# The first step of a hybrid decoder layer: one interleaved chain of products for 512 tokens, or four chains of 128 tokens each

## The chip, the cores and the metric

The kernel runs on one core of a Trainium2 chip. The core has a matrix engine (TensorE, PE in the profile; its weight loads are PEld), a vector engine (VectorE, DVE), a scalar engine (ScalarE, ACT), a general engine (GpSimd, POOL) and an engine that issues most DMAs (SyncE, SP). PE, DVE and ACT work between two on-chip memories: SBUF, with 128 partitions, and PSUM, with eight banks of 128x512 float32 into which PE writes. The metric is the device time of one execution in microseconds.

## What is computed

One decoder layer on 1024 tokens of width 1024, in float32. The change touches only the beginning of it, the normalization and the large input projection:

```python
def rms_norm(x, g):
    xf = x.astype(jnp.float32)
    y = xf * lax.rsqrt(jnp.mean(xf * xf, axis=-1, keepdims=True) + NORM_EPS)
    return (y * g.astype(jnp.float32)).astype(x.dtype)

def hybrid_layer(x, layer_idx, pre_g, post_g, w_in, ...):
    h = rms_norm(x, pre_g)
    z = jnp.einsum('bsd,de->bse', h, w_in)
    qa, ka, va, ga, qb, kb, vb, gb, gk_low = split_columns(z)
    ...
```

Behind it come causal differential softmax attention (8 heads), chunked gated linear attention (4 heads), gates, and an output projection with a second normalization and the residual.

## The kernel before

**Products in three terms.** Every float32 operand of a large product is split into a high part, rounded to a narrower format (a copy, on ACT mostly), and a low part, the operand less the high part (a subtraction, on DVE). A product is then hi*hi + hi*lo + lo*hi. In the profile `h_hi`, `s_hi`, `w` are written by CAST, COPY or ACTIVATE on ACT, their low parts by TENSOR_TENSOR on DVE. One call of `mm` (L144) is one product of a 128x128 stationary and a 128x512 moving operand; `tr` (L147) is a transpose of 128x128.

**Seven products for eight.** The projection of a column group is done on 2x2 blocks, tokens in halves of 512 and width in halves of 512, with a scheme of Strassen's kind: steps n = 1 to 7 of a column group p multiply one combination of activation blocks (h11, h12, h22, s1 to s4) by one combination of weight blocks (b11, b12, b21, b22). Step n=1 is h11 times b11, n=2 is h12 times b21, n=5 is s1 times b12 - b11, n=6 s2 times b11 - b12 + b22 (built up in place), n=7 s3 times b22 - b12. The list `order` sets which (p, n) follow each other: (0,1), (1,1), (0,2), (1,2), (2,1), (2,2), then n = 5, 6, 7, 4 for p = 0 and 1 in turn. Columns p = 0 and 1 are the values of the gated part: there the tokens are the stationary operand, one PSUM bank for each of four tiles of 128 tokens (the results x and y in the profile; their sums go out as gv_st through `take_gated`). p = 2 is the first ordinary group; its weights come through `w_early`.

**The first step.** `load_x` (L675) loads x in eight tiles of 128 tokens. SP's queue holds x0 to x3, b11's first half, pre_g, b11's second half, x4 to x7, b21, w_early. `norm_x` takes the mean square of a tile (ACT, into `junk`; for tile 3 half of it on DVE), adds eps (DVE), takes the power -0.5 (POOL, `ssq`), and `scale_x` multiplies the tile by it (DVE). `first(0)` transposes the first 512 columns of the four tiles into four banks, one bank for each 128 columns, with spins (products of zeros) between to fill PE's wait; `put` multiplies by pre_g, by now along partitions, while it makes the high part (ACT) and the low part (DVE). `gated_first` then runs the products of all four tiles interleaved: 16 of w_hi with h_hi, 16 of w_hi with h_lo, then `first(1)`, 16 transposes for the other half of the columns (h12, through the float copy `f1`, in the profile f), then 16 with w_lo.

**The second half of the tokens.** `blocks(j)`, for j = 0 to 3, transposes column block j and j+4 of tiles 4 to 7 (8 transposes), scales them with pre_g (ACT, the tiles t21 and t22, both t in the profile) and makes s1 = h21 + h22 (DVE). blocks(0) stands ahead of (0,2), blocks(1) behind it, blocks(2) behind (1,2), blocks(3) behind (2,1). `differences(j)` then makes h21 = h11_hi - h21, adds h11_lo, and s2 = h22 less that, all on DVE. s4 = f1 - s2 follows in front of (0,7), again on DVE.

**What sets the order.** The engines run in order. PE's instructions keep the program's order. While `pinned[0]` is set, the instructions of ACT, DVE and POOL keep it too (L56 to L59); later ones are placed by a scheduler, with `tc.issue_after` as hints. `hold` limits how far `prepare` may make weights ahead, and `between` keeps pieces of work for a later place. `free` hands PSUM banks out in turn.

Of the kernel before, what the change touches and what calls it, by code (L numbers as in the profile page):

```python
# [31 lines left out]
def hymba_kernel(  # L32
# [288 lines left out]
    def gated_weights(n):  # L321
# [26 lines left out]
        if n == 1:  # L348
            for k in range(2):
                dve.tensor_copy(w[0][:, k], src[0][:, k])  # L350
            between[:] = [
                lambda: lo(1),
                lambda: (scale_x(3, cols(1)), lo(0)),
                lambda: act.copy(w[1][:, 1], src[1][:, 1]),
                lambda: (act.copy(w[1][:, 0], src[1][:, 0]), scale_x(2, cols(1))),
                lambda: [scale_x(st, cols(1)) for st in range(2)],
            ]
# [1489 lines left out]
```

## Time and profile before

| what | value |
| --- | --- |
| median of 3 runs | 961.26 us (960.8 to 961.41) |
| the profiled execution | 960.34 us |
| its span, from the first to the last instruction | 958.6 us |
| PE, PEld busy | 948.2 us (99%), 793.2 us (83%) |
| DVE, ACT, POOL busy | 742.3 us (77%), 604.7 us (63%), 193.9 us (20%) |
| TensorE clock granted | 0.998 |

The span stands 1.74 us below the profiled execution's time; 1.74 us lie around it. All durations come from this one execution. Busy shares are means over the whole span; the change concerns its first 80 us. In rows of the timeline the first number is the start in microseconds from the span's start and the second the length; "x4" counts instructions, and in brackets stands how long the engine was idle before the row and which engine's work ended that.

### The profile page before, as it was taken

To read this page: it belongs to the slowest core of one execution; us is meant where nothing else is said; L and a number is where in the kernel's file an instruction comes from. 1 tells how busy PE (TensorE), PEld (TensorE's weight loads), DVE (VectorE), ACT (ScalarE), POOL (GpSimd) and SP (SyncE) were. 2 spreads that over 40 slices of the span, in tenths; PEclk is the share of its full clock that TensorE was granted. 3 is DMA by queue.
4 is the path that set the end of the run, shared out by engine and by line. 5 is a ranking of instruction groups with operands and counts; after the bars stand their busy time and mean duration, and the time that the engine had idled before them with its cause. 6 is when DMAs were issued, how large, how long until landed. Compare 5 with 4: busy or idle time off the path is not lost.

```text
span 958.6 us, 14358 instructions
## 1 busy us (share of the span) xinstructions
PE 948.2 (99%) x4624; PEld 793.2 (83%) x4624; DVE 742.3 (77%) x1476; ACT 604.7 (63%) x1162; POOL 193.9 (20%) x263
## 2 busy tenths in 40 slices
PE   9999999999999999999999999999999999999997
PEld 7877788888888888888888888888888888888885
DVE  5998799996778787687767476588888888898464
ACT  7753355845777556577765444366677677787773
POOL 2001002222141112131100002122222222433321
PEclk9999999999999999999999999999999999999999
DMA  8546367487577897986755498996665679994776
GB/s 285 162 149 172 91 203 244 168 293 249 188 255 242 275 305 255 295 258 216 263 175 154 143 298 265 411 291 217 220 223 193 222 230 349 331 291 105 160 206 141
DMA packets 153258, 220.34 MB, mean 230 GB/s; under 512 B 15776, under 2 KB 85664, under 8 KB 153088
## 3 DMA queue, kind: packets, MB, share of 16 engines
q1 hardware_dynamic: 138736, 177.65, 57.8%
q0 software_dynamic: 14448, 41.79, 14.8%
q8 instruction: 36, 0.59, 0.3%
q14 instruction: 38, 0.31, 0.1%
HBM read 133.93 MB, written 88.60 MB: 232 GB/s over the span
## 4 chain that ended last, share of the span: by engine, by line
PE 96%; DVE 1%; ACT 1%; DMA 1%; issue 0%; POOL 0%; SPq 0%; DVEq 0%; ACTq 0%
PE x L144 23%; PE z L144 16%; PE y L144 16%; PE ypart L144 14%; PE sc L144 7%; PE po L144 5%; PE yps L144 4%; PE wtr L147 3%; PE gpo L144 3%; PE kv L144 1%; PE gkl_ps L144 1%; PE pa L144 1%; PE xT L147 1%; DMA x<-in_x_dram 1%; PE ms L144 0%; PE pk L147 0%
## 5 line engine op out<-in xcount | busy, mean ns | idle before, releaser
L66 ACT CAST w<-w_raw 128x512 fp32r<-128x512 f32 x138 | 85.1, 620 | 70.0 <-PE y L144 31.7
L66 ACT ACTIVATE p<-p,stt 128x896 f32<-128x896 f32 (+7 forms) x128 | 99.3, 777 | 30.8 <-DVE stt L66 29.9
L66 DVE TENSOR_TENSOR w<-w_raw,w 128x512 fp32r<-128x512 f32 x138 | 94.0, 684 | 31.5 <-ACT w L66 31.4
L66 ACT COPY s<-x 128x512 f32<-128x512 f32 x78 | 44.7, 584 | 65.1 <-PE x L144 64.9
L66 DVE CUSTOM_DVE_ANT_0 p<-sc,maskt 128x512 f32<-128x512 f32 (+3 forms) x128 | 74.2, 585 | 14.5 <-PE sc L144 13.2
L66 POOL TENSOR_SCALAR p<-p,stt,lam 128x1024 f32<-128x1024 f32 (+3 forms) x64 | 55.9, 874 | 143.9 <-DVE stt L66 143.8
L144 PE MATMUL z<-s_hi,w 128*128 128x512 f32 x320 | 80.1, 393 | 0.0
L144 PE MATMUL x<-s_hi,w 128*128 128x512 f32 x320 | 80.0, 392 | 0.0
L144 PE MATMUL y<-h_hi,w 128*128 128x512 f32 x320 | 80.0, 392 | 0.0
L144 PE MATMUL ypart<-wo_hi,m_hi 128*128 128x512 f32 x192 | 79.5, 414 | 0.1
L144 PE MATMUL ypart<-wo_hi,m_lo 128*128 128x512 f32 x192 | 75.5, 393 | 0.0
L144 PE MATMUL ypart<-wo_lo,m_hi 128*128 128x512 f32 x192 | 75.4, 393 | 0.0
L66 POOL DMA_DIRECT2D wo_d<-wo_hi x32 | 17.4, 543 | 270.4 <-ACT wo_hi L66 270.4
L144 PEld LDWEIGHTS z<-s_hi,w 128*128 128x128 f32 x320 | 59.8, 188 | 12.3
L144 PEld LDWEIGHTS x<-s_hi,w 128*128 128x128 f32 x320 | 59.7, 188 | 12.3
L144 PEld LDWEIGHTS y<-h_hi,w 128*128 128x128 f32 x320 | 59.7, 188 | 12.2
L144 PE MATMUL sc<-k,q 128*128 128x512 f32 (+1 forms) x192 | 68.9, 362 | 0.1
L144 PE MATMUL sc<-ks,q 128*128 128x512 f32 (+1 forms) x192 | 66.1, 347 | 0.0
L66 ACT CAST wt_hi<-wtr 128x512 fp32r<-128x512 f32 (+1 forms) x80 | 42.8, 534 | 29.0 <-PE wtr L147 28.3
L66 DVE TENSOR_TENSOR wt_lo<-wtr,wt_hi 128x512 fp32r<-128x512 f32 (+1 forms) x80 | 50.6, 633 | 9.9 <-ACT wt_hi L66 9.1
L66 DVE TENSOR_TENSOR w_raw<-w_raw 128x512 f32<-128x512 f32 x80 | 56.2, 703 | 1.4 <-DMA w_raw<-in_w_in_dram 0.4
L66 DVE TENSOR_TENSOR c<-z,s 128x512 f32<-128x512 f32 x48 | 32.8, 687 | 31.3 <-ACT s L66 19.3
(234 smaller groups left out, 2348.0 us busy)
## 6 DMA issues: line engine op xcount, KB each, us to landing
w_raw<-in_w_in_dram SPq DMA_DIRECT2D x40, 512.0 KB, 4.9
wo_d<-wo_hi POOLq DMA_DIRECT2D x32, 256.0 KB, 3.0
q<-q_d SPq DMA_DIRECT2D x32, 256.0 KB, 5.3
k<-k_d SPq DMA_DIRECT2D x32, 256.0 KB, 5.5
ks<-k_d SPq DMA_DIRECT2D x64, 128.0 KB, 6.2
wo_raw<-in_w_out_dram POOLq DMA_DIRECT2D x31, 256.0 KB, 5.0
v<-v_d SPq DMA_DIRECT2D x14, 512.0 KB, 7.7
wo_d<-gqd POOLq DMA_DIRECT2D x22, 256.0 KB, 4.1
```

Source lines behind the costliest of these rows:

```text
L66: ins = op(*a, **k)
L144: tc.keep_in_program_order(pe.matmul(*a, **k))
L147: tc.keep_in_program_order(pe.transpose(dst, src, ident))
```

## The change

**Loads.** SP's queue now holds x0, g_bc, x1, b11 in both halves, x2, x3, x4, pre_g, b21, x5 to x7, w_early. g_bc is new: the first 512 numbers of the pre-norm weights, broadcast to 128 partitions (256 KB).

**Four chains.** Each tile of 128 tokens goes through the start by itself: mean square, power, one DVE instruction that multiplies its first 512 columns by the norm and by g_bc (`scale_g`), four transposes into one bank (`turn_x`), two casts of 128x2x128 for the high part (`put_hi`), two subtractions for the low part (`put_lo`), and twelve products into its own bank (`products`). Tile 1's transposes stand behind four products of tile 0. b11's low part is made on DVE between tile 1's and tile 2's. `second_half` (formerly `first(1)`) follows tile 3's transposes; its 16 transposes stand ahead of tile 3's twelve products.

**The rest.** The squares of tiles 5, 6 and 7 come behind the casts of h12. Tiles 6 and 7 are scaled by ACT. blocks(0) moves into step (1,2), behind its first chain, blocks(1) behind that step, blocks(2) and blocks(3) behind (2,1). The low weights of (0,5) are made behind blocks(3). The four additions of h11_lo in `differences` and the four subtractions from f1 go from DVE to POOL. The casts of s4 get a hint that places them behind the weight casts of (0,7).

At PE's start before, all transposes come first (`x_188` holds tiles 0 and 1, `x_191` tiles 2 and 3):

```order
L144 MATMUL spin<-idle,ones 128x512 x13
L147 MATMUL xT<-ident,x_188 128x128 x4
L144 MATMUL spin<-idle,ones 128x512 x3
L147 MATMUL xT<-ident,x_188 128x128 x4
L144 MATMUL spin<-idle,ones 128x512 x5
L147 MATMUL xT<-ident,x_191 128x128 x8
L144 MATMUL spin<-idle,ones 128x512
L144 MATMUL x<-w,h_hi 128x512 x16
L144 MATMUL x<-w,h_lo 128x512 x16
```

PE's start with the change (`x_199` holds tiles 2 and 3):

```order
L144 MATMUL spin<-idle,ones 128x512 x13
L147 MATMUL xT<-ident,x_188 128x128 x4
L144 MATMUL spin<-idle,ones 128x512 x5
L144 MATMUL x<-w,h_hi 128x512 x2
L144 MATMUL x<-w,h_lo 128x512 x2
L147 MATMUL xT<-ident,x_188 128x128 x4
L144 MATMUL x<-w,h_hi 128x512 x2
L144 MATMUL x<-w,h_lo 128x512 x2
L144 MATMUL x<-w,h_hi 128x512 x4
L144 MATMUL x<-w,h_lo 128x512 x4
L144 MATMUL x<-w,h_hi 128x512 x4
L147 MATMUL xT<-ident,x_199 128x128 x4
```

Products of tile 0 now stand ahead of the transposes of the other tiles, and tile 1's products ahead of tile 2's transposes.

On DVE from the first sum s1 of `blocks` before (`t_416` is t21, `t_417` t22, `s_428` and `s_492` the first two sums, `g_raw<-g_raw` the subtractions b12 - b11, gv_st the sums of y and x):

```order
L66 TENSOR_TENSOR s_428<-t_416,t_417 128x512
L66 TENSOR_TENSOR g_raw<-g_raw 128x1024
L66 TENSOR_TENSOR w<-w_early,w 128x512 x2
L66 TENSOR_TENSOR gv_st<-y,s 128x512
L66 TENSOR_TENSOR g_raw<-g_raw 128x1024
L66 TENSOR_TENSOR t_416<-h_hi,t_416 128x512
L66 TENSOR_TENSOR s_lo<-s_428,s_hi 128x512
L66 TENSOR_TENSOR gv_st<-y,s 128x512
L66 TENSOR_TENSOR w<-g_raw,w 128x1024
L66 TENSOR_TENSOR s_492<-t_416,t_417 128x512
L66 TENSOR_TENSOR t_416<-h_lo,t_416 128x512
L66 TENSOR_TENSOR gv_st<-y,s 128x512
```

The same place with the change (`t_459` is t21, `t_460` t22):

```order
L66 TENSOR_TENSOR gv_st<-y,s 128x512 x2
L66 TENSOR_TENSOR w<-w_early,w 128x512 x2
L66 TENSOR_TENSOR s_491<-t_459,t_460 128x512
L66 TENSOR_TENSOR g_raw<-g_raw 128x1024 x2
L66 TENSOR_TENSOR gv_st<-y,s 128x512
L66 TENSOR_TENSOR t_459<-h_hi,t_459 128x512
L66 TENSOR_TENSOR gv_st<-y,s 128x512
L66 TENSOR_TENSOR s_lo<-s_491,s_hi 128x512
L66 TENSOR_TENSOR w<-g_raw,w 128x1024
L66 TENSOR_TENSOR s_535<-t_459,t_460 128x512
L66 TENSOR_TENSOR w<-g_raw,w 128x1024
```

The first two gv_st now stand ahead of the first sum, the third behind the sum and both g_raw subtractions, and the additions of h_lo (`t_416<-h_lo,t_416`) are no longer there.

On POOL, from the two last powers to the first large fill, with the change (before, the two DMAs and the MEMSET followed each other, with nothing between):

```order
L66 TENSOR_TENSOR ssq<-ssq,eps_t 128x2 x2
L66 TENSOR_TENSOR t_459<-h_lo,t_459 128x512 x2
L66 DMA gk_up<-in_w_gk_up_dram 16x512
L66 TENSOR_TENSOR t_459<-h_lo,t_459 128x512 x2
L66 DMA wd<-in_w_in_dram 128x8x16
L66 TENSOR_TENSOR s_624<-f_353,s_624 128x512 x2
L66 TENSOR_TENSOR s_625<-f_353,s_625 128x512 x2
L66 MEMSET gkl 128x1024
```

The eight operations taken from DVE stand there. The core of the diff:

```diff
-            if name == "b11" and not i:
-                sp.dma_start(pre_g, pre_norm_g[0].rearrange("(k p) -> p k", p=P))
...
+            if (p, n) == (GATED[1], 2) and us == (0,):
+                blocks(0)
...
-    def gated_first():
+    def products(u, w, terms, ks=range(HB)):
+        hi, lo = H["h11"]
+        for j in terms:
+            a, part = ((0, hi), (0, lo), (1, hi))[j]
+            for k in ks:
+                mm(
+                    units[u]["x"], at(part, k)[:, u * P : u * P + P], w[a][k // 2][:, k % 2, :],
...
+    def scale_g(st):
+        x_cs = xs[st][:, cols(0)]
+        dve.scalar_tensor_tensor(x_cs, x_cs, norms[st], g_bc, ALU.mult, ALU.mult)
+    def turn_x(u):
+        ps, i = take_bank([P, 512], "xT")
+        for k in range(HB):
+            tr(ps[:, k * P : (k + 1) * P], xs[u][:, k * P : (k + 1) * P])
...
+    load_x(0)
+    g_bc = hw.tile([P, 512], F32, tag="s1_hi1", name="g_bc")
+    sp.dma_start(g_bc, pre_norm_g[0:1, :512].to_broadcast([P, 512]))
+    load_x(1)
     gated_tiles("b21")
     load_gated("b11")
-    for st in range(4, 8):
+    for st in range(2, 5):
         load_x(st)
+    sp.dma_start(pre_g, pre_norm_g[0].rearrange("(k p) -> p k", p=P))
     load_gated("b21")
+    for st in range(5, 8):
+        load_x(st)
...
+    open_unit()
+    products(0, w_first, (0, 1), (0, 1))
+    ps = turn_x(1)
+    products(0, w_first, (0, 1), (2, 3))
+    put_hi(ps, 1)
+    square(2)
+    low_weights(0)
+    put_lo(ps, 1)
+    low_weights(1, slice(0, 1))
+    power(2)
+    low_weights(1, slice(1, 2))
+    open_unit()
+    products(1, w_first, (0, 1))
+    products(0, w_first, (2,))
+    square(3)
+    scale_g(2)
+    ps = turn_x(2)
+    products(1, w_first, (2,))
...
-        dve.tensor_tensor(h21, fp(at(lo, j)), h21, ALU.add)
+        pool.tensor_tensor(h21, fp(at(lo, j)), h21, ALU.add)
...
+    second_half()
+    open_unit()
+    products(3, w_first, (0, 1, 2))
+    square(5)
+    power(4)
...
+    for st in (6, 7):
+        act.activation(xs[st], xs[st], AF.Copy, scale=norms[st])
...
-            with tc.issue_after(s3_lo.ins):
-                dve.tensor_tensor(s, f1[:, j], s, ALU.subtract)
+            pool.tensor_tensor(s, f1[:, j], s, ALU.subtract)
...
+            with tc.issue_after(casts[1]):
+                behind = [parts("s4", j, s24[i][:, j % 2], None if i else lows[7])]
```

Left out here are the split of `norm_x` into `square` and `power`, and one hint in the attention scores, which changes no place in any engine's row.

More of the change, by code (lines that the diff above doesn't have):

```diff
@@ L348, in gated_weights @@
         if n == 1:
[L349 to L357, printed above, removed]
             return w[:2], w[2:]
         hi(0)
-        if n == 7:
+        if n in (5, 7):
             hi(1)
-            casts.append(act.latest)
+            if n == 7:
+                casts.append(act.latest)
             between.append(lo)
@@ L703, in norm_x, with square, power @@
-        pool.tensor_tensor(ssq[:, 1], ssq[:, 2], mhalf[:, :n], ALU.pow)
-    for st in range(4):
-        load_x(st)
+            norms[st] = ssq[:, 1, i : i + 1]
+            squares[st] = ssq[:, 0, i : i + 1]
+        roots[sts[0]] = ssq
+    def square(st, c=D):
+        junk = hw.tile([P, D], F32, tag=("s2_hi0", "s2_lo0")[st % 2], name="junk")
+        act.activation(
+            junk[:, :c], xs[st][:, :c], AF.Square, scale=D**-0.5, accum_out=squares[st]
+        )
+        return junk
+    def power(st):
+        ssq = roots[st]
+        dve.tensor_scalar(ssq[:, 2], ssq[:, 0], EPS, None, ALU.add)
+        pool.tensor_tensor(ssq[:, 1], ssq[:, 2], mhalf[:, : ssq.shape[2]], ALU.pow)
@@ new lines, in hymba_kernel, with low_weights @@
+    hold[0] = 2
+    prepare(0)
+    prepare(1)
+    (w_hi, w_lo), b11 = ws.pop(0), gated_raws["b11"]
+    ws.pop(1)
+    w_first = (w_hi, w_lo)
+    def low_weights(i, ks=slice(0, 2)):
+        dve.tensor_tensor(w_lo[i][:, ks], b11[i][:, ks], fp(w_hi[i][:, ks]), ALU.subtract)
+    pinned[0] = True
+    square(0)
+    power(0)
+    square(1)
+    scale_g(0)
+    scale_x(0, cols(1))
+    power(1)
+    spin(13)
+    ps = turn_x(0)
+    spin(5)
+    put_hi(ps, 0)
+    for k in range(2):
+        dve.tensor_copy(w_hi[0][:, k], b11[0][:, k])
@@ new lines, in hymba_kernel @@
+    put_lo(ps, 0)
+    scale_g(1)
+    for k in range(2):
+        act.copy(w_hi[1][:, k], b11[1][:, k])
+    open_unit()
[15 more added lines that the diff above has]
+    ps = turn_x(2)
@@ L840, in go @@
                     fill.pop(0)
-    for i in range(2):
-        prepare(i)
-    first(0)
-    norm_x(4, 5)
-    for st in (4, 5):
-        scale_x(st, slice(0, D))
-    between.pop()()
-    norm_x(6, 7)
-    for st in (6, 7):
-        scale_x(st, slice(0, D))
+    made[0] = 2
     hold[0] = 4
@@ L854, in hymba_kernel @@
         prepare(i)
-    hold[0] = 8
-    step(0)
+    second_half()
+    open_unit()
+    products(3, w_first, (0, 1, 2))
+    square(5)
+    power(4)
+    square(6)
+    square(7)
+    for st in (4, 5):
+        scale_x(st, slice(0, D))
+    power(6)
+    go(1)
+    for st in (6, 7):
+        act.activation(xs[st], xs[st], AF.Copy, scale=norms[st])
+    pinned[0] = False
+    hold[0] = 6
     t21, t22 = (
@@ L860, in hymba_kernel @@
     )
-    blocks(0)
     go(1)
     blocks(1)
+    hold[0] = 8
     go(1)
     blocks(2)
-    go(1)
     sums_done = blocks(3)
+    w_lo = between.pop()
+    for i in range(2):
+        w_lo(i)
     go(1)
@@ L1333, in scores @@
                 behind = tc.issue_after(lowest[0]) if forced else nullcontext()
-                with behind:
+                row = tc.issue_after(read[-1]) if h == 0 and qb == 5 and read else nullcontext()
+                with behind, row:
                     ins = dve.tensor_tensor_reduce(
```

117 lines of the change are left out of this document (48 added, 69 removed).

## The prediction

> **What bounds the kernel now.** I read the page's first part, then what PE waited for, then the chain in order of time over the first 80 us. The page's span and its PE row:
>
> ```profile
> span 958.6 us, 14358 instructions
> PE 948.2 (99%) x4624; PEld 793.2 (83%) x4624; DVE 742.3 (77%) x1476; ACT 604.7 (63%) x1162; POOL 193.9 (20%) x263
> ```
>
> The view of waits for PE has three rows (total, times, longest):
>
> ```profile
> PE spin L144 <- POOL idle L66: 1.5, 1, 1.5
> PE x L144 <- DVE w L66: 0.8, 1, 0.8
> PE xT L147 <- DVE x L66: 0.7, 1, 0.7
> ```
>
> TensorE is busy 99% of the span. The change leaves its products as they are, so it can only move the moment of the first product, remove the 0.8 us wait, or add waits. The chain of waits in order of time (start, length) gives the pace:
>
> ```profile
> 1.71 5.82 DMA x<-in_x_dram
> ...
> 12.07 7.59 PE x L144 x32
> 19.67 1.75 PE xT L147 x16
> 21.41 3.65 PE x L144 x16
> 25.06 0.87 PE xT L147 x8
> 25.93 5.46 PE y L144 x24
> ```
>
> A product of 512 columns takes 5.46 / 24 = 0.2275 us, a transpose 0.87 / 8 = 0.109. The first product starts at 12.07, behind all four token tiles. These rows of the timeline price the small steps (start, length, count; consecutive records overlap, so a step is shorter than a single record):
>
> ```profile
> 6.22 0.49 DVE L66 TENSOR_SCALAR x<-x,ssq 128x512 f32<-128x512 f32 x1 [0.70 <-POOL ssq L66]
> 6.91 0.60 PE L147 MATMUL xT<-ident,x 128*128 128x128 f32 x4
> 11.08 0.76 DVE L66 CAST w<-g_raw 128x512 fp32r<-128x512 f32 x2
> 18.83 2.02 ACT L66 CAST w<-g_raw 128x1024 fp32r<-128x1024 f32 x2
> 20.75 2.42 ACT L66 ACTIVATE f<-xT,pre_g 128x512 f32<-128x512 f32 x4
> 23.04 2.20 ACT L66 CAST h_hi<-f 128x512 fp32r<-128x512 f32 x4
> 25.69 2.07 PE L144 MATMUL y<-w,h_hi 128*128 128x512 f32 x8
> 31.87 1.27 ACT L66 ACTIVATE t<-xT,pre_g 128x512 f32<-128x512 f32 x2
> 33.71 0.68 DVE L66 TENSOR_TENSOR gv_st<-y,s 128x512 f32<-128x512 f32 x1
> 46.80 1.89 DVE L66 TENSOR_TENSOR s<-t,t 128x512 f32<-128x512 f32 x3
> 48.60 2.35 DVE L66 TENSOR_TENSOR g_raw<-g_raw 128x1024 f32<-128x1024 f32 x2
> 66.05 2.49 DVE L66 TENSOR_TENSOR s<-f,s 128x512 f32<-128x512 f32 x4
> 72.07 3.02 PE L144 MATMUL x<-w,s_hi 128*128 128x512 f32 x12 [0.78 <-DVE w L66]
> ```
>
> So DVE steps are (1.89 - 0.68) / 2 = 0.60 for 512 columns and 1.13 for 1024. Rows of the groups by form give DVE's multiply of three operands and a 256-column subtraction (0.42, step about 0.40):
>
> ```profile
> L66 DVE SCALAR_TENSOR_TENSOR c<-c,qk_hi 128x512 fp32r<-128x512 f32 x28 | 18.8, 684 | 1.3 <-ACT qk_hi L66 1.1
> L66 DVE TENSOR_TENSOR wo_lo<-wo_raw,wo_hi 128x256 fp32r<-128x256 f32 x20 | 7.5, 418 | 1.3 <-ACT wo_hi L66 1.3
> ```
>
> **1, the start.** The view of DMA issues gives the first tile and b11's first half (microseconds to landing; issued 0.80 and 2.65, so landed at 4.20 and 10.05):
>
> ```profile
> x<-in_x_dram SPq DMA_DIRECT2D x1, 512.0 KB, 3.4
> g_raw<-in_w_in_dram SPq DMA_DIRECT2D x1, 512.0 KB, 7.4
> ```
>
> That half is the fifth load of 512 KB: 2.0 MB in 5.85 us after the first, 0.34 MB per us. With the change 256 KB of g_bc, x1 and the half itself follow x0, 1.25 MB, so it lands at 4.20 + 3.7 = 7.9, say 8.0. Tile 0 is ready by then: its transposes stood at 6.91 and move by the longer multiply, 0.68 against 0.49, to 7.1. Then DVE in order: two casts of b11 (0.42 and 0.34), two low halves (0.80), tile 1's scaling (0.68): tile 1's transposes start at 10.24. PE has had four products by then. From there to y it has 44 products (10.01) and 28 transposes (3.05), 13.07 in all: y at 23.31 without a wait. Before, y stood at 25.69 behind blocks(0)'s eight transposes (0.87), which now come later, so the equal mark is 24.82: 1.5 ahead.
>
> Tile 2's transposes will wait. DVE runs b11's low parts and tile 1's lows (1.13, 0.80, 0.60) ahead of tile 2's mean, then POOL takes the power, DVE the scaling. That ends at 14.65, against PE's 14.32, if POOL runs beside DVE's next subtraction, and at 15.25 if behind it: 0.3 to 0.95, taken as 0.6. Lead: **0.9**.
>
> **2, y behind the second half.** y's products need the h12_hi casts. On ACT stand, from tile 3's transposes: 0.65 until they are out, two hi casts of 256 columns (no such row; 0.36 each, between 0.30, half the 512 cast, and 0.59), b21's casts 1.94, f 2.29, first h12_hi 0.67: 6.27. PE has four products, 16 transposes and 12 products to do: 0.44 for tile 3, 0.91, 1.74 and 2.73, or 5.82. It waits 0.45, then the next three casts come every 0.51 against 0.2275 a product, 0.85 more. Before, ACT began f at 20.75, 4.9 ahead of y, and y waited for nothing. Cost **1.3** (0.8 to 1.8).
>
> **3, x(2,1) behind gv_st.** Its bank comes free with the third gv_st, which now stands on DVE behind the first sum and both subtractions of b12. From blocks(0)'s start: transposes and two scalings on ACT end at 1.91, the sum 0.60 and hand-overs to 2.6, g_raw 2 x 1.13, gv_st 0.68: 5.53. PE has 0.87 + 2.73 + 0.87 = 4.47. Cost **1.07** (0.5 to 1.4).
>
> **4, adds on POOL.** Four adds of h_lo and four subtractions from f1 leave DVE, 0.60 each, and go to POOL. POOL's nearest rows, by tile (ns min/median/max), then instances in the timeline, two beside DVE's two-operand instructions and one pair beside a DVE instruction that reads one operand from PSUM:
>
> ```profile
> L66 POOL TENSOR_SCALAR_AFFINE_SELECT gan<-gan x8: 647/1566/6864, 233.7 to 489.0; 128x512 f32<-128x512 f32 x8
> L66 POOL TENSOR_TENSOR gate<-r,gate x14: 1292/1297/1607, 675.1 to 895.0; 128x512 f32<-128x512 f32 x14
> ```
>
> ```profile
> 271.10 6.86 POOL L66 TENSOR_SCALAR_AFFINE_SELECT gan<-gan 128x512 f32<-128x512 f32 x1
> 271.36 0.69 DVE L66 TENSOR_TENSOR w<-w_raw,w 128x512 fp32r<-128x512 f32 x1
> ...
> 276.78 0.69 DVE L66 TENSOR_TENSOR w<-w_raw,w 128x512 fp32r<-128x512 f32 x1
> 344.51 0.86 POOL L66 TENSOR_SCALAR_AFFINE_SELECT gan<-gan 128x512 f32<-128x512 f32 x1
> 344.79 1.12 DVE L66 TENSOR_TENSOR go<-go,gg 128x512 fp32r<-128x512 f32 x1
> 675.05 1.29 POOL L66 TENSOR_TENSOR gate<-r,gate 128x512 f32<-128x512 f32 x1 [2.16 <-DVE stt L66]
> 675.62 0.68 DVE L66 TENSOR_TENSOR wt_lo<-wtr,wt_hi 128x512 fp32r<-128x512 f32 x1
> ```
>
> The same instruction takes 0.65 alone and 6.86 while DVE's two-operand subtractions follow each other; where POOL is in first, DVE's 0.68 becomes 1.12, a loss of 0.44. Nearly all neighbours of the new adds read both operands from SBUF. An add is twice the 0.65, so its toll p on DVE is taken as 2 x 0.43 = 0.86; the ends are 0.44 and the whole 1.30. [...]
>
> Laid end to end, with adds of 1.30 and no toll, DVE is idle for 0.5 at each of the first two, and POOL's h_lo adds must reach s2. z(0,5) needs s1_lo's third piece 15.47 after blocks(0)'s start and DVE has it at 15.05, a slack of 0.42; two tolls beyond the idle cost 2 x (0.86 - 0.5) = 0.7. Cost **0.3** (0 to 1.2). x(0,7) needs b12's subtraction and cast, 33.45 against PE's 34.58, a slack of 1.1. Five adds fall before it, with 1.5 of DVE's idle to hide in: 5 x 0.86 - 1.5 = 2.8, less 1.1 and the 0.3 already lost: **1.4** (0 to 2.7).
>
> **5, the old wait.** In x(0,7) PE stood 0.78 for w's low part, behind four subtractions (2.49) that POOL now has. Without toll that wait goes. With 0.86 the low part is ready 5.5 after x(0,7)'s start against a need at 4.75, so 0.8 of waiting stays: **0** against before. After it the order of every engine is the old one, so what is gained or lost by then stays to the end.
>
> **Cheap edits.** g_bc, the spins, the squares of tiles 5 to 7 (ACT, under y) and xt6's and xt7's scalings (ACT instead of DVE) lie under PE's 5.5 us of y; uncovered, the ACT work (3.2 plus 2.1) would hold blocks(0) by up to 1. On SP's queue b21 passes x5 to x7; x7 is then the end of 5.75 MB behind x0, at 0.34 landed by 21.1, and its square comes behind the h12_hi casts, near 24. pre_g, moved behind x4 (3.25 MB, 13.8), is first used by f near 20. The wait put on the scores changes no place in DVE's order: nothing, either way.
>
> **Sum.** -0.9 + 1.3 + 1.07 + 0.3 + 1.4 + 0 = +3.2 us. The profiled execution took 960.34 (958.6 of span and 1.74 around it), so 963.5 by it; it stood 0.9 under the median of 961.26, so 964.5 on that. About 0.2%, 1.9 us, is what a measurement tells here from no change. All low ends together (-1.2 + 0.8 + 0.5 - 0.78) make -0.7, all high ones (-0.55 + 1.8 + 1.4 + 1.2 + 2.7 + 0.9) +7.4; they don't come all at once, and +1.5 to +5.7 is kept for the forecast's own.
>
> **The rivals.** First, not slower: POOL's adds run beside DVE (p under 0.5), as 14 gate multiplications of 1.30 did with DVE at 0.68. Then tile 2 waits 0.3, the tolls are nothing and the old wait goes: -1.2 + 1.3 + 1.07 - 0.78 = +0.4, 961.7, within the 0.2%. Against it: those neighbours had an operand in PSUM, which the new ones don't. It decides at p = 0.5, where DVE's idle is used up.
>
> Second, faster: the lead is kept whole, since ACT's casts go at their lower ends and gv_st gets its turn in time: -1.5 - 0.78 = -2.3, 959.0. For it: PE waited for no cast in before's y. Against: 2 and 3 are made of rows that hardly vary. It decides where 2 and 3 fall under 0.4 together.
>
> Third, a lock: POOL's add holds DVE for its whole 1.30, as far as the 0.71 lost once by a DVE instruction of 0.69 beside an AFFINE_SELECT of 0.65 goes:
>
> ```profile
> 307.24 1.40 DVE L66 TENSOR_TENSOR w_raw<-w_raw 128x512 f32<-128x512 f32 x1
> 307.44 0.65 POOL L66 TENSOR_SCALAR_AFFINE_SELECT gan<-gan 128x512 f32<-128x512 f32 x1
> ```
>
> Then -0.55 + 1.3 + 1.07 + 1.2 + 2.7 + 0.9 = +6.6, 967.9. Against it: the 0.44.
>
> **How the numbers follow.** The forecast 0.40, the first rival 0.32, the second 0.18, the third 0.10. The second gives faster, 0.18. The first, and 0.05 of the forecast whose terms fall at their low ends, give the same, 0.37. The rest is slower, 0.45. The range runs from the second rival, 959.0, to 967.0, a microsecond past the forecast's high terms; half of the second and most of the third lie outside, under 0.2. The forecast alone has 962.8 to 967.0.
>
> **What would show it.** In the changed profile: the first product near 8.5; tile 1's transposes near 10.2 and a wait there; PE's waits naming ACT h_hi under y (1.3), DVE gv_st under x(2,1) (1.1), ACT w or DVE w under x(0,7) (1.4 and 0.8). POOL's adds well over 1.3, or DVE's 0.68 rows at 1.1 to 1.5 around them, would show the toll; adds at 1.30 with DVE at 0.68 would show the first rival. The forecast is wrong if PE's waits after 24 us sum to under 2, or if y starts before 23.5.

## The result and the profile after

The changed kernel takes 968.72 us (median of 5 runs, 968.35 to 970.29) against 960.8 for the kernel before (5 runs, 960.23 to 961.41): a ratio of 1.0088, interval 1.0075 to 1.0100. It is 7.9 us slower; 3.2 had been forecast. The profiled execution took 968.68 with a span of 966.6, 8.0 more than before, at a granted clock of 0.999.

Of the page, the span and PE's row, and of the view of waits those of PE (total, times, longest):

```profile
span 966.6 us, 14372 instructions
PE 949.9 (98%) x4620; PEld 791.3 (82%) x4620; DVE 743.6 (77%) x1468; ACT 606.8 (63%) x1168; POOL 213.0 (22%) x271
```

```profile
PE x L144 <- ACT w L66: 2.5, 1, 2.5
PE z L144 <- DVE s_lo L66: 1.6, 2, 0.9
...
PE x L144 <- DVE gv_st L66: 0.9, 1, 0.9
```

The largest that are new beside the waits of before are those for ACT w, DVE s_lo and DVE gv_st. Where they stand is read from PE's timeline (start, length). First the kernel after, then the kernel before at four of these places:

```profile
10.10 0.74 PE L144 MATMUL x<-w,h_hi 128*128 128x512 f32 x2 [0.59 <-DVE w L66]
...
25.59 2.96 PE L144 MATMUL y<-w,h_hi 128*128 128x512 f32 x8
...
40.30 2.11 PE L144 MATMUL x<-h_hi,w 128*128 128x512 f32 x8 [0.91 <-DVE gv_st L66]
...
47.63 1.07 PE L144 MATMUL z<-w,s_hi 128*128 128x512 f32 x4
...
61.67 1.98 PE L144 MATMUL x<-w,s_hi 128*128 128x512 f32 x8
...
75.17 2.33 PE L144 MATMUL x<-w,s_hi 128*128 128x512 f32 x8 [2.46 <-ACT w L66]
...
86.41 1.98 PE L144 MATMUL y<-w,h_hi 128*128 128x512 f32 x8
```

```profile
38.36 2.07 PE L144 MATMUL x<-h_hi,w 128*128 128x512 f32 x8
...
44.79 1.98 PE L144 MATMUL z<-w,s_hi 128*128 128x512 f32 x8
...
55.67 1.98 PE L144 MATMUL x<-w,s_hi 128*128 128x512 f32 x8
...
78.55 1.98 PE L144 MATMUL y<-w,h_hi 128*128 128x512 f32 x8
```

The starts of the same step give an account of the shift. Up to x(2,1) the kernel before has one block of eight transposes more behind it, so 0.87 is taken off its marks there (25.69 and 38.36).

| PE reaches | before | after | shift | added in the stretch | forecast for it |
| --- | --- | --- | --- | --- | --- |
| y of (0,2) | 24.82 | 25.59 | +0.77 | +0.77 | -0.9 |
| x of (2,1) | 37.49 | 40.30 | +2.81 | +2.04 | +1.3 and +1.07 |
| z of (0,5) | 44.79 | 47.63 | +2.84 | +0.03 | 0 |
| x of (0,6) | 55.67 | 61.67 | +6.00 | +3.16 | +0.3 |
| y of (0,4) | 78.55 | 86.41 | +7.86 | +1.86 | +1.4 and 0 |
| end of span | 958.6 | 966.6 | +8.0 | +0.1 | 0 |

Everything is lost in the first 86 us. The chain of waits in order of time tells more than PE's waits do. Before, from 55.83 to 78 us (start, length):

```profile
55.83 9.08 PE x L144 x40
...
64.92 1.22 DVE g_raw L66
...
70.88 1.15 DVE w L66
...
72.07 6.65 PE x L144 x28
```

From the first product at 12.07 up to 64.91 that chain is PE's own. After, from blocks(0) on:

```profile
37.29 1.29 DVE g_raw L66 x2
...
50.95 2.78 DVE s_lo L66 x2
...
66.86 3.19 DVE s_lo L66 x3
...
72.90 1.15 DVE g_raw L66
...
74.07 1.05 ACT w L66
...
75.17 11.40 PE x L144 x48
```

From the first sum of blocks(0), at 36.68, to the wait at 75.17 the chain lies on DVE, with two short links on ACT; PE is not on it at all. The windows agree (in each row the stretch, its length, busy time of PE, PEld, DVE, ACT, POOL with instructions, clock, DMA share, GB/s). Before:

```profile
27.00:36.00 9.00, 9.00 (x46) 7.53 (x45) 9.00 (x13) 6.65 (x12) 0.00 (x0) 1.00 0.61 184
...
46.00:56.00 10.00, 10.00 (x46) 8.29 (x45) 9.31 (x15) 4.90 (x7) 0.00 (x0) 1.00 0.44 130
```

After:

```profile
27.00:36.00 9.00, 8.98 (x44) 7.47 (x44) 5.41 (x10) 8.03 (x15) 1.39 (x2) 1.00 0.31 101
...
46.00:56.00 10.00, 7.91 (x32) 5.34 (x32) 10.00 (x13) 5.00 (x9) 6.63 (x5) 1.00 0.46 141
56.00:66.00 10.00, 10.00 (x46) 8.28 (x45) 10.00 (x15) 3.25 (x4) 6.22 (x1) 1.00 0.67 213
```

DVE's 77% of the whole span hides a stretch in which it never pauses. Before, it is busy 9.00 of 9 us in 27 to 36, since the first sum stands at 27.83. After, it idles for 3.6 of those 9 us, because blocks(0) comes later, and from 46 to 66 it is busy 20.00 of 20. The share alone does not part the two kernels: from 36 to 76 DVE is busy 37.4 of 40 us before and 38.6 after, but before, PE is busy 39.2 of the same 40, and after, 34.5.

What POOL did to it is seen in DVE's and POOL's rows of the changed kernel:

```profile
40.92 1.30 POOL L66 TENSOR_TENSOR t<-h_lo,t 128x512 f32<-128x512 f32 x1 [9.49 <-DVE t L66]
41.36 1.40 DVE L66 TENSOR_TENSOR s_lo<-s,s_hi 128x512 fp32r<-128x512 f32 x1
...
46.77 2.38 DVE L66 TENSOR_TENSOR s<-t,t 128x512 f32<-128x512 f32 x2
49.84 3.35 POOL L66 TENSOR_TENSOR t<-h_lo,t 128x512 f32<-128x512 f32 x2 [1.16 <-DVE t L66]
50.87 2.86 DVE L66 TENSOR_TENSOR s_lo<-s,s_hi 128x512 fp32r<-128x512 f32 x2
59.78 12.57 POOL L66 TENSOR_TENSOR s<-f,s 128x512 f32<-128x512 f32 x4 [5.67 <-DVE s_lo L66]
66.86 6.04 DVE L66 TENSOR_TENSOR s_lo<-t,s_hi 128x512 fp32r<-128x512 f32 x4 [0.77 <-ACT s_hi L66]
```

A single DVE row of this kind takes 0.68, a pair 1.28, four in a row 2.50. So DVE lost 0.72, 1.10 and 1.58 around the four adds, 3.40 in all or **0.85 an add**, and 3.54 on the row of four beside the subtractions, **0.89 each**: 6.9 for eight. POOL's four subtractions stretched from 5.2 (4 x 1.30) to 12.57: POOL's row began at 59.78, the DVE rows up to 66.1 kept their lengths (2.48 for four of 512 columns, 2.35 for two of 1024), and DVE lost time only behind its own pause of 0.77 at 66.1. DVE's 0.85 and 0.89 are two thirds of POOL's 1.30, not the whole. No run shows by what the two engines hold each other up.

### The profile page after: what moved, and what is told of

Its sections match the earlier page's. It is cut to its first block, busy times and chain, and to the rows that moved or that the text cites. A ratio compares the mean times of both kernels' runs of the same rounds, so it can differ in the third digit from the quotient of the medians.

```text
span 966.6 us, 14372 instructions
## 1 busy us (share of the span) xinstructions
PE 949.9 (98%) x4620; PEld 791.3 (82%) x4620; DVE 743.6 (77%) x1468; ACT 606.8 (63%) x1168; POOL 213.0 (22%) x271
## 4 chain that ended last, share of the span: by engine, by line
PE 92%; DVE 4%; ACT 1%; issue 1%; DMA 1%; POOL 0%; SPq 0%; DVEq 0%; ACTq 0%
PE x L144 22%; PE y L144 15%; PE z L144 15%; PE ypart L144 14%; PE sc L144 7%; PE po L144 5%; PE yps L144 4%; PE wtr L147 3%; PE gpo L144 3%; PE kv L144 1%; DVE s_lo L66 1%; PE gkl_ps L144 1%; PE pa L144 1%; DMA x<-in_x_dram 1%; DVE s L66 1%
## 5 line engine op out<-in xcount | busy, mean ns | idle before, releaser
L144 PE MATMUL sc<-ks,q 128*128 128x512 f32 (+1 forms) x192 | 66.1, 347 | 0.0
```

What stands on the lines that cost most here:

```text
L144: tc.keep_in_program_order(pe.matmul(*a, **k))
```

## The experiments

Sixteen kernels were run. Each ratio is to executions of the kernel before taken beside it. Three of them leave something out or compute other numbers, and only their times count: e5 scales by numbers that are not the pre-norm weights, e11 leaves these weights out for the first 512 columns of the first 512 tokens, and e13 leaves the low part of h11 out of the differences.

| run | edit | median us | ratio (interval) |
| --- | --- | --- | --- |
| e1_adds_dve | after; the adds on DVE | 969.43 | 1.0089 (1.0074 to 1.0104) |
| e2_subs_dve | after; the subtractions on DVE | 965.88 | 1.0056 (1.0041 to 1.0071) |
| e3_both_dve | after; both on DVE | 965.12 | 1.0048 (1.0031 to 1.0064) |
| e4_g_by_pe | after; g_bc made by PE | 971.38 | 1.0107 (1.0092 to 1.0122) |
| e5_g_rows | after; g_bc loaded from 128 rows | 968.0, one run | none |
| e6_g_by_pe_warm | after; g_bc made by PE, earlier | 968.66 | 1.0084 (1.0069 to 1.0099) |
| e7_b21_early | e3; b21's casts ahead of tile 3's | 964.25 | 1.0041 (1.0026 to 1.0055) |
| e8_gv_first | e3; third gv_st ahead of b12 - b11 | 964.98 | 1.0046 (1.0031 to 1.0061) |
| e9_late_diffs | e3; differences behind the last s1 | 966.62 | 1.0063 (1.0048 to 1.0079) |
| e10_three | e3 with the edits of e7, e8, e9 | 964.91 | 1.0046 (1.0033 to 1.0058) |
| e11_no_g_load | e10; g_bc not loaded | 963.40 | 1.0030 (1.0018 to 1.0041) |
| e12_g_behind | e10; weights multiplied behind the transposes | 965.68 | 1.0054 (1.0042 to 1.0066) |
| e13_no_adds | e3; the adds left out | 962.62 | 1.0023 (1.0014 to 1.0033) |
| e14_subs_early | e3; b12 - b11 in DVE's idle time | 963.55 | 1.0033 (1.0021 to 1.0045) |
| e15_subs_b21 | e14 with the edit of e7 | 962.60 | 1.0022 (1.0013 to 1.0032) |
| e16_blocks_early | e15; blocks(0) ahead | 962.89 | 1.0029 (1.0018 to 1.0041) |

### POOL's eight operations

**e1.** The four adds go back:

```diff
-        pool.tensor_tensor(h21, fp(at(lo, j)), h21, ALU.add)
+        dve.tensor_tensor(h21, fp(at(lo, j)), h21, ALU.add)
```

> The changed kernel (968.72 us) with only the four additions of h11_lo back on DVE; the four subtractions from f1 stay on POOL. [...] Back on DVE they cost 4 x 0.60 = 2.4 there and these losses go, and s2 no longer waits for POOL: the stalls in z(0,5), 3.1 us now, fall to about 1.5, total near 967. Rival, the order: z(0,5) waits because blocks(2) and blocks(3) come later than before, whichever engine adds; 2.4 us more on DVE then make it the same or up to 1 slower, 968.7 to 969.7.

No gain: 969.43, where 967 had been forecast on DVE's losses around the adds (0.72, 1.10 and 1.58) going. (0,5) took 12.37 instead of 14.04, so its wait shrank from 3.1 to 1.45. But POOL's subtractions now began at 58.11, and DVE paid for them there, 4.54 for a pair of low weights that takes 2.35 in the kernel after:

```profile
58.11 8.95 POOL L66 TENSOR_TENSOR s<-f,s 128x512 f32<-128x512 f32 x4 [6.57 <-DVE s_lo L66]
...
61.38 4.54 DVE L66 TENSOR_TENSOR w<-g_raw,w 128x1024 fp32r<-128x1024 f32 x2
```

Then PE waited 1.04 in (0,6) and 2.32 in (0,7). Against e3, which has the same DVE rows without POOL's, those from the second lot of s_lo to the end of h_lo end 4.1 later (69.4 and 65.3), about 1.0 for each of POOL's four operations. So the toll goes with POOL's operations: this time other DVE instructions paid it. Of this execution's 970.0, some 1.4 belong to a fall of TensorE's clock to 0.50 behind the wait of 2.32, shown in the last section.

**e2.** The four subtractions go back, the adds stay on POOL:

```diff
-            pool.tensor_tensor(s, f1[:, j], s, ALU.subtract)
+            with tc.issue_after(s3_lo.ins):
+                dve.tensor_tensor(s, f1[:, j], s, ALU.subtract)
```

> The changed kernel with only the four subtractions from f1 back on DVE, behind the last s3_lo as before; the additions stay on POOL. Theory of the lock: four s_lo of 6.04 us in all (2.49 before) and POOL's 12.57 for four subtractions are one and the same; without them DVE's subtraction of b12 and the cast behind it come 3.5 earlier, PE's 2.46 wait at x(0,7) goes, and the old 0.8 wait inside x(0,7) returns: near 967.0. Rival, the order: the b12 subtraction is late because everything on DVE is late since z(0,5); the 2.46 wait stays and 2.4 more on DVE add the old wait: 969.5.

2.8 us less than the kernel after, and the 2.46 wait is gone. On POOL they had run as soon as their inputs were there, beside the DVE work ahead of x(0,7)'s weights; on DVE they stand behind the subtraction that makes these weights, which now begins at 69.24 instead of 72.83.

**e3.** Both edits.

> The changed kernel with all eight operations back on DVE, so no work on POOL beside DVE there. Theory of the lock: the gains of the two single steps add up, near 965.3, PE's waits after 47 us under 2.5. Rival, the order: 969 to 970.5, with the waits in z(0,5) and x(0,7) as long as now.

965.12, 3.6 less than the kernel after. That is the price of the eight operations on POOL, and 4.3 to 4.4 us of the loss are left without them. The tolls account for it: 3.54 beside the subtractions, and 3.40 beside the adds less the 2.4 that the adds cost on DVE, make 4.5, and the subtraction for x(0,7)'s weights begins 4.35 earlier in e3 (68.48 against 72.83). DVE now works from the first sum to x(0,7)'s low weights (start, length), and PE waits for the last of it:

```profile
36.71 0.69 DVE L66 TENSOR_TENSOR s<-t,t 128x512 f32<-128x512 f32 x1 [1.21 <-ACT t L66]
...
75.50 1.22 DVE L66 TENSOR_TENSOR w<-g_raw,w 128x1024 fp32r<-128x1024 f32 x1
```

```profile
76.77 3.02 PE L144 MATMUL x<-w,s_hi 128*128 128x512 f32 x12 [0.88 <-DVE w L66]
```

The kernel before has the first sum at 27.83, the end of the same low weights at 72.01 and PE's row at 72.07. In e3 PE's row is 4.7 later, the span 4.6 longer.

### The start

**e4.** g_bc is loaded as one row of 2 KB and spread to 128 partitions by one product with a row of ones, behind the spins:

```diff
-    sp.dma_start(g_bc, pre_norm_g[0:1, :512].to_broadcast([P, 512]))
+    sp.dma_start(g_bc[0:1], pre_norm_g[0:1, :512])
...
+    g_ps, g_i = take_bank([P, 512], "g_ps")
+    spin(13)
+    mm(g_ps, fp(ones)[0:1, :], g_bc[0:1], start=True, stop=True)
...
-    spin(13)
```

> The changed kernel with g_bc made on chip: one row of 2 KB is loaded, PE multiplies it by a row of ones into a bank (one product of 512 columns between the spins), and the scaling reads it from PSUM. Theory: the broadcast load moves 256 KB at 123 to 225 GB/s between 3 and 6 us and holds up x1 and b11 behind it; without it tile 0 is scaled at about 6.1 instead of 6.88 and the first half of b11 lands about 1.6 earlier, so the first product starts near 8.5 instead of 10.10 and tile 1's transposes near 10.2 instead of 11.66; kept to the end it is 967.2. Rival: what is ahead at the start is lost again at y, which waits for ACT's casts of h12, and at x(2,1): under 0.5 us of it stay, 968.3 or more.

2.7 slower than the kernel after, and not for the reason in question: the granted clock, eighth column, was 0.50 from 9 to 12 us, behind the small product:

```profile
9.00:10.00 1.00, 1.00 (x4) 0.88 (x4) 0.61 (x2) 0.55 (x3) 0.68 (x1) 0.50 1.06 404
10.00:11.00 1.00, 1.00 (x4) 0.74 (x3) 0.87 (x3) 1.00 (x3) 0.00 (x0) 0.50 1.00 401
11.00:12.00 1.00, 1.00 (x4) 0.81 (x3) 1.00 (x2) 0.13 (x1) 0.00 (x0) 0.50 1.04 356
```

The first product came at 11.34, and the first sum at 37.69, 1.0 later than in the kernel after. A second loss stood behind the wait ahead of (0,7), here 2.51: the eight products there took 3.22 instead of 2.33, and y(0,4) began at 88.93 against 86.41, another 1.5. The run says nothing on the load.

**e5.** The same 256 KB, from 128 different rows of w_in instead of one row read 128 times:

```diff
-    sp.dma_start(g_bc, pre_norm_g[0:1, :512].to_broadcast([P, 512]))
+    sp.dma_start(g_bc, w_in[0, :P, :512])
```

> The changed kernel with g_bc's 256 KB read from 128 different rows of w_in in place of one row of pre_norm_g 128 times (so the tokens are scaled by other numbers; only its time is read). Theory: the load is slow because all 128 packets of 2 KB read the same 2 KB; with different rows the 16 DMA engines move over 340 GB/s between 3 and 6 us, x1's mean square starts near 7.0 instead of 8.18 and the first product near 9.0 instead of 10.10; about 967.6. Rival: any 256 KB ahead of x1 costs this; rates, starts and time stay as they are, 968.7.

The DMA issues (KB each, microseconds to landing), first of the kernel after, then of e5. x0 was issued at 0.80 and landed 3.2 and 3.3 later; g_bc was issued at 1.24, x1 at 1.71 and 1.70:

```profile
g_bc<-in_pre_norm_g_dram SPq DMA_DIRECT2D x1, 256.0 KB, 5.5
x<-in_x_dram SPq DMA_DIRECT2D x1, 512.0 KB, 6.4
```

```profile
g_bc<-in_w_in_dram SPq DMA_DIRECT2D x1, 256.0 KB, 3.7
x<-in_x_dram SPq DMA_DIRECT2D x1, 512.0 KB, 5.6
```

From one row g_bc lands 2.7 behind x0 (6.7 less 4.0), from 128 rows 0.8 (4.9 less 4.1). The forecast had 0.75. In the meantime the queues are busy and move little; the window of the kernel after (DMA share and GB/s at the end of the row), and the same one before:

```profile
4.00:5.00 1.00, 1.00 (x4) 0.81 (x3) 0.00 (x0) 0.97 (x2) 0.00 (x0) 1.00 0.87 123
```

```profile
4.00:5.00 1.00, 1.00 (x4) 0.81 (x3) 0.00 (x0) 0.81 (x1) 0.00 (x0) 1.00 0.95 352
```

With e5's rows the first product came at 9.22 instead of 10.10 and y at 24.78 instead of 25.59, so 0.8 of the start is the broadcast's. The execution's span, 965.9, is 0.7 shorter, although PE had a slow stretch in (0,5), where 16 products took 5.41 instead of 3.84:

```profile
53.56 5.41 PE L144 MATMUL z<-w,s_hi 128*128 128x512 f32 x16
...
74.37 2.33 PE L144 MATMUL x<-w,s_hi 128*128 128x512 f32 x8 [0.90 <-ACT w L66]
```

Those 1.57 came off the wait ahead of (0,7), 0.90 here and 2.46 in the kernel after. PE's lost time cost nothing there, because DVE's work, which began 0.8 earlier, set when the wait ended.

**e6.** e4 with the small product between two lots of spins, seven and four.

> As the run with g_bc made by PE, but the product with the row of ones stands between 7 and 4 spins, so that neither it nor a gap behind it leaves TensorE idle long, and g is ready before tile 0's power is. Theory: the clock of 0.50 from 9 to 12 us was what made that run slow; with it at 1.00 the first product stands near 8.9, tile 1's transposes near 10.4 instead of 11.66, y's start near 24.4 instead of 25.59, and the gain of 1.2 stays to the end: 967.5. Rival: the gain is lost at y's stall behind ACT's casts or in z(0,5): 968.3 or more.

The mean granted clock of the profiled execution was 0.999 (0.996 in e4), but no time was gained: 968.66. The small product took 2.07, and x1 landed at 7.8 although only 2 KB stood ahead of it (8.1 in the kernel after). The first product came at 10.76. Why x1 was no earlier than that is open, so a short load ahead is not by itself the cure.

**e11 and e12** stand on e10, below, where PE's waits from y to (0,5) are gone. e11 leaves the load out and fills g_bc with ones:

```diff
-    sp.dma_start(g_bc, pre_norm_g[0:1, :512].to_broadcast([P, 512]))
+    pool.memset(g_bc, 1.0)
```

> The kernel of the three moves with no load for g_bc at all: the tile is filled with ones by POOL, which leaves the pre-norm weights out of the first 512 columns of the first 512 tokens. Theory: without it x1 lands at 5.4 as before and b11's halves at 7.0 and 8.3, the first product stands near 8.2 and tile 1's transposes near 9.5, 2.0 ahead of the changed kernel; 2.0 less than the three moves' time, 960.2 by theory. Rival: the start then waits for tile 2's and 3's means instead, and under 1.0 of it stays: 961.3 or more.

The first product came at 8.95 (10.03 in e10), y at 24.11 (25.58), and 1.5 us were kept to the end, 963.40 against 964.91. In this kernel, what the start loses, the end loses.

**e12** multiplies by pre_g behind the transposes, as the kernel before did, eight rows coming over POOL's queue and being transposed on PE:

```diff
-        dve.scalar_tensor_tensor(x_cs, x_cs, norms[st], g_bc, ALU.mult, ALU.mult)
+        dve.tensor_scalar(x_cs, x_cs, norms[st], 1.0, ALU.mult, ALU.mult)
...
-            act.copy(tokens(H["h11"][0], u, k), ps[:, 2 * k : 2 * k + 2])
+            act.activation(
+                tokens(H["h11"][0], u, k // 2)[:, k % 2], ps[:, k], AF.Copy, scale=pre_g[:, k : k + 1]
+            )
```

> The kernel of the three moves with the pre-norm weights multiplied behind the transposes again, by 128 columns (four operations on ACT and four on DVE for each tile in place of two and two), and loaded as 8 rows of 512 bytes by POOL's queue and turned by one transpose, so that neither the broadcast nor the load of single numbers stands in SP's queue. Theory: tile chains are up to 0.5 longer, the loads 2 us shorter, so it keeps 1.5 of what the kernel without any load keeps: 960.7. Rival: the eight operations of each tile on ACT and DVE take the place of the loads, and it is no faster than the three moves alone: 962.2.

0.8 slower than e10: y began at 26.87, with a wait of 1.34 for the eight rows and 0.72 for a low part. The small load was not early either, and the low part now comes in four pieces of 128 columns where it came in two of 256.

### PE's waits, one by one

**e7** puts b21's casts ahead of tile 3's on ACT:

```diff
+    hold[0] = 4
+    for i in (2, 3):
+        prepare(i)
...
-    hold[0] = 4
-    for i in (2, 3):
-        prepare(i)
```

> The kernel with all eight operations back on DVE (965.12) with b21's two casts and low parts moved ahead of tile 3's casts, into ACT's idle time before tile 3's transposes. Theory: y's first eight products, 2.98 us instead of 2.07, wait for h12_hi behind b21's casts (2.0 us on ACT ahead of f); without them there f starts near 21.5 instead of 22.60, the stall of 0.9 and the 0.2 ahead of y go: 964.1. Rival: the casts then hold up tile 3's own casts, or b21 hasn't landed at 18.7, and the time stays within 0.4 of 965.1.

The wait under y went (PE's first eight products of y take 1.98 instead of 2.96), the first sum came at 35.63 instead of 36.71, and y(0,4) 1.1 earlier than in e3 (82.16). The span is 0.7 shorter, the median 0.9; by the intervals alone e3 and e7 aren't told apart.

**e8** puts the subtractions of b12 - b11 behind the third gv_st on DVE (`gvs` is a new list of the gv_st additions in their order):

```diff
-                dve.tensor_tensor(src[i], a[i], b[i], ALU.subtract)
+                with tc.issue_after(gvs[2].ins) if n == 5 else nullcontext():
+                    dve.tensor_tensor(src[i], a[i], b[i], ALU.subtract)
```

> The kernel with all eight operations back on DVE (965.12) with the subtractions b12 - b11 placed behind the third gv_st. Theory: x(2,1)'s wait of 0.9 is for that gv_st alone; it goes, and 964.2 is left. Rival: the two subtractions (2.26 us) then delay b12's weights and the sums behind them on DVE, and z(0,5) waits longer by what x(2,1) gained: 965.1.

The 0.9 wait under x(2,1) went, and came back under z:

```profile
PE z L144 <- DVE s_lo L66: 1.7, 2, 1.1
```

That wait was 0.9 in e3. (0,6) began at 60.06 against 60.09: nothing kept.

**e9** makes the four differences behind the last s1:

```diff
-        dve.tensor_tensor(h21, fp(at(hi, j)), h21, ALU.subtract)
-        pool.tensor_tensor(h21, fp(at(lo, j)), h21, ALU.add)
         with tc.issue_after(sums_done.ins):
+            dve.tensor_tensor(h21, fp(at(hi, j)), h21, ALU.subtract)
+            dve.tensor_tensor(h21, fp(at(lo, j)), h21, ALU.add)
```

> The kernel with all eight operations back on DVE (965.12) with every operation of the differences (h11_hi - h21, + h11_lo) placed behind the last s1 of the second half. Theory: what is left of z(0,5)'s stall, 12.4 us from its start to x(0,6) against 10.92 of work, is DVE's order: blocks(2) and (3) stand late and three subtractions and three additions stand ahead of their s1_lo; behind them z loses under 0.5: about 964.0. Rival: the differences are then late for s2, and x(0,6) or x(0,7) waits for what z gained: 965.1.

(0,5) took 10.89, no wait left, and the kernel became 1.5 slower than e3. DVE, with its differences held back, now paused four times for ACT; two of the four rows:

```profile
45.57 0.69 DVE L66 TENSOR_TENSOR s<-t,t 128x512 f32<-128x512 f32 x1 [0.48 <-ACT t L66]
46.73 0.69 DVE L66 TENSOR_TENSOR s<-t,t 128x512 f32<-128x512 f32 x1 [0.47 <-ACT t L66]
```

With 0.18 and 0.33 beside them these are 1.46 of idle time, and the span is 1.5 longer. The wait of 1.5 taken from PE gained nothing, and the pauses of 1.5 on DVE cost all of themselves.

**e10** has all three edits.

> The kernel with all eight operations back on DVE (965.12) with three moves at once: b21's casts ahead of tile 3's, the subtractions b12 - b11 behind the third gv_st, the differences behind the last s1. Theory: each wait is an order on ACT or DVE and they add up once nothing behind eats them: y 0.9, x(2,1) 0.9, z 1.1, so 962.2. Rival: DVE is the bound of this stretch, so what one move gains the next wait takes, and only b21's 0.9 stays: 964.2.

964.91, as good as e3. The view names no wait of PE from y to (0,5), then 0.31 in (0,6) and 1.22 and 0.88 in (0,7).

### What bounds the stretch from 36 to 77 us

**e13** leaves the four adds out of e3; the products and their order stay.

> The kernel with all eight operations back on DVE (965.12) with the four additions of h11_lo left out altogether, so that the differences lack the low part of h11 (only its time is read). Theory: DVE's work between the first sum of the second half and x(0,7)'s low weights is the bound, 40.0 us without a gap; 4 x 0.60 = 2.4 less work there is 2.4 less in the end: 962.7. Rival: ACT's casts or the order of the waits is the bound; then z(0,5) loses up to 1.0 less and x(0,7) waits for its weights as before: 964.2 or more.

962.62, 2.5 less than e3; four instructions at a step of 0.60 are 2.4. Taking work off DVE pays in full, where taking PE's waits in x(2,1) and (0,5) paid nothing.

**e14** uses DVE's idle time ahead of the first sum: b12 is loaded before step (0,2), and its subtractions stand right behind that step:

```diff
-            if a:
+            if a and n != 5:
...
+    load_gated("b12")
     go(1)
+    for a, b in zip(gated_raws["b12"], gated_raws["b11"]):
+        dve.tensor_tensor(b, a, b, ALU.subtract)
```

> The kernel with all eight operations back on DVE (965.12) with b12's load issued by the program and its two subtractions of b11 made right behind step (0,2), where DVE is idle, instead of behind the first sum. Theory: 2.26 us of work leave the bound stretch, x(2,1)'s wait of 0.9 goes with them: 962.9. Rival: b12 hasn't landed by 33, or the idle time was not what was lost, and the next wait takes the gain: 964.5 or more.

1.6 less than e3 by the medians, of 2.26 moved. The subtractions went into the gap, to 33.12, and the low weights of (0,7) start at 74.31 instead of 75.50, 1.2 earlier; the two profiled spans differ by 1.1. DVE has a new pause:

```profile
58.77 0.69 DVE L66 TENSOR_TENSOR s_lo<-s,s_hi 128x512 fp32r<-128x512 f32 x1 [0.69 <-ACT s_hi L66]
```

That pause of 0.69 and a first sum 0.19 later (36.90) took most of the rest.

**e15** adds e7's edit.

> The same with b21's casts ahead of tile 3's as well. Theory: the first sum comes 1.0 earlier, since y has no stall, and DVE's stretch starts from there: 961.9, within 0.2% of the kernel before. Rival: the stretch is not DVE's; then the two gains (1.0 and what the run before gives) do not add up.

962.60, another 0.95: what e7 gave by itself is added in full, since it starts DVE's work earlier.

**e16** puts blocks(0) right behind (0,2).

> The same with blocks(0) right behind step (0,2), ahead of (1,2). Theory: tiles 6 and 7 are scaled by 33.7 at the earliest, so PE waits about 1.7 ahead of blocks(0), which costs nothing while DVE is the bound; the first sum comes 1.1 earlier, but the two low parts of w_early (1.3) then fall into the stretch: 961.9, no better. Rival: PE's time counts, and its new wait of 1.7 adds to the end: 963.5.

962.89, no better. PE now waits 0.7 for ACT's scaling of tiles 6 and 7. The first sum came 1.7 earlier than in e15, at 34.19, but x(0,7)'s low weights only 0.2 earlier.

**The runs together.** If DVE's row of work bounds the stretch, then the moment at which it has x(0,7)'s low weights (start plus length of that row) sets the span. Both columns are differences to the kernel before, 72.01 and 958.6:

| run | first sum at | low weights ready at | later by | span longer by |
| --- | --- | --- | --- | --- |
| e2 | 36.61 | 77.47 | 5.5 | 5.5 |
| e3 | 36.71 | 76.72 | 4.7 | 4.6 |
| e7 | 35.63 | 75.63 | 3.6 | 3.9 |
| e8 | 36.72 | 76.72 | 4.7 | 4.6 |
| e9 | 36.59 | 78.24 | 6.2 | 6.1 |
| e10 | 35.68 | 76.37 | 4.4 | 4.3 |
| e11 | 34.21 | 74.94 | 2.9 | 3.1 |
| e12 | 36.97 | 77.70 | 5.7 | 5.1 |
| e13 | 36.71 | 74.31 | 2.3 | 2.3 |
| e14 | 36.90 | 75.53 | 3.5 | 3.5 |
| e15 | 35.89 | 74.52 | 2.5 | 2.4 |
| e16 | 34.19 | 74.33 | 2.3 | 2.4 |

The last two columns agree within 0.3 in eleven of the twelve, through runs that removed waits of PE (e8, e9, e10) and runs that removed work of DVE (e13, e14). In e12 the span is 0.6 shorter than the mark says; it was regained behind 108 us, and how is open. The table holds the runs with the four subtractions on DVE. With these on POOL the mark is another one: in the kernel after, the low weights are ready at 76.38, 4.4 later than before, and the span is 8.0 longer, because there PE already waited 2.46 for the high part of the same weights, whose subtraction on DVE stood behind the tolls.

No version came under the kernel before; e15 is nearest among those that compute everything, 0.22% slower. What is left in it, about 2 us, has no experiment of its own: e11's edit on top of e15 was not tried, nor blocks(0) back ahead of (0,2).

## Why the prediction was wrong, step by step

The direction was right, the size was not: 968.72 lies above the whole range. By the account above the forecast missed 1.7 at the start and 2.9 + 0.5 in (0,5) and in (0,6) with (0,7), and was 0.3 too dear on the way to x(2,1).

**Step 1, the start, is the first that failed.** It put g_bc's 256 KB at the 0.34 MB per us of x's and b11's loads. Those read different rows; a broadcast reads one row 128 times, and took 2.7 where 0.75 had been taken. b11's half landed at 9.5 instead of 8.0, the first product came at 10.10 instead of 8.5, tile 1's transposes at 11.66 instead of 10.24, y at 25.59 instead of 23.9. The forecast of the wait ahead of tile 2's transposes, 0.3 at its low end, was met (0.32). e5 shows the broadcast's share: with other rows the half landed at 8.7 and the first product came 0.9 earlier. The other 0.7 is not the broadcast's: in e5 too the loads behind g_bc came slower than 0.34 MB per us, and why is open. A term was left out besides: tile 1's mean stands ahead of b11's casts on DVE and waits for x1, and in the kernel after it ended at 9.51, as late as the half landed. By e11, in the kernel of e10, what the start loses is kept to the end.

**Step 2, y behind the second half, held**: the products of y stood 0.52 apart where 0.51 had been worked out,

```profile
25.59 0.50 PE y L144
...
26.11 0.49 PE y L144
```

which with 0.18 ahead of them makes 1.1, against 1.3. PE's wait view does not name ACT h_hi there, though the prediction had expected it; only the length of the row shows it. **Step 3** held too, 0.91 against 1.07.

**Step 4, the adds on POOL, is the second that failed, and not in its price.** The toll had been taken as 0.86 an operation, and 0.85 and 0.89 were measured. What failed is the count and the cover. Two tolls were counted ahead of (0,5)'s third piece, each with 0.5 of DVE's idle time to hide in. All four adds' tolls fell before it, and DVE had no idle time: 3.4 less the slack of 0.42 is 3.0, and (0,5) lost 3.16. For x(0,7) five of the eight operations were counted; all eight came first, because POOL took the subtractions as soon as their inputs stood (its row at 59.78). The slack of 0.42, the only part of this that rests on DVE's order alone, is borne out by e3: three adds on DVE, 1.8 less 0.42, make 1.4 there, and (0,5) lost 1.5. The 0.65 that the prediction took for POOL's instruction alone is the row at 307.44, beside a DVE row of 1.40; no row shows its length without such a neighbour.

**Step 5**: the old wait for the low weights had been forecast to stay, and went; the 2.46 ahead of (0,7) gave DVE the time for them. The two steps together added 1.86, for a forecast of 1.4.

**Beneath both lies the step that was not taken.** The working priced PE's waits, one after the other, with a slack for each. The chain of before already ran over DVE from 64.92 to 72.03, and PE's 0.78 wait for `DVE w` was its end: DVE had no slack at that place, and the first sum of blocks(0), where its work begins, was being moved from 27.83 to past 36. In such a stretch a term counts by what it does to DVE, not to PE: a later first sum, a pause, a toll. e8 and e9 show the difference, and so does e5, where 1.57 lost by PE cost nothing.

**The rivals.** The first and the second needed cheap neighbours or a kept lead; neither was there. The third, the lock, named 967.9, the nearest number. Its terms behind the start make 7.2, the measured ones 7.1, but it had too high a toll, 1.30, on too few operations, and the start 1.3 too early. That the eight operations cost more on POOL than on DVE is shown by e3 against the kernel after, with 3.6 us.

## What to carry to other kernels

Read the busy share of each engine in the stretch that a change touches, not in the span: an engine at 77% overall was 92 to 100% busy for 40 us. In the kernel before it was 92 to 97% busy there and PE was still the bound up to 64.91, so the share is a warning and the chain of waits in order of time the test. Once the chain lies on such an engine, its first instruction, its pauses and its amount of work set the time, and waits removed from the engine behind it come back at the next place, as the 0.9 in e8 did. Before work is handed to POOL, count the two-operand DVE instructions that will stand beside it; here each operation of 1.30 on POOL cost DVE 0.85 to 1.0 to save it 0.60.

## What the runs showed of the hardware

**The clock fell behind waits of 0.91 and 2.32 us, and not behind others of 1.14 and 2.46.** In e1's profiled execution the wait of 2.32 in (0,7) was followed by products at half the clock:

```profile
74.92 3.52 PE L144 MATMUL x<-w,s_hi 128*128 128x512 f32 x8 [2.32 <-ACT w L66]
```

```profile
76.00:77.00 1.00, 1.00 (x4) 0.71 (x4) 0.50 (x2) 1.00 (x4) 0.00 (x0) 0.50 0.00 0
```

In e4 the eight products behind a wait of 2.51 took 3.22. In the kernel after (2.46) and in e6 (2.50) they took 2.33, and in the kernel after the clock stayed at 1.00. In e5, with waits of 0.60 and 0.95 in (0,5), 16 products took 5.41 at a mean clock of 0.996; in the kernel after, behind the same waits, they took 3.84 at 1.00. What made the clock fall in some executions and not in others is open. Behind the product of one row in e4, with a wait of 0.91, it fell to 0.50 as well; in the kernel after, which has no such product, a wait of 1.14 at that place left it at 1.00. The five times of the kernel after lie in two groups, 968.35 to 968.72 and 970.0 to 970.29, and the slower products at (0,7) cost 1.5 in e4; whether such a loss parts the groups is open, since only one of the five was profiled. The mean clocks (0.996 to 0.999) do not settle it: in e5 the mean was 0.996, and the slow products ahead of a wait cost no time.

**The broadcast from one row was a slow load.** 256 KB landed 2.7 us behind the load ahead of it where 128 rows took 0.8, with the DMA engines 79% to 87% busy at 123 to 225 GB/s from 3 to 6 us, and x1 behind it landed at 8.1 instead of 7.3 in e5.
